# One masked 128x128 tile of probabilities per query block, and the recurrent branch in two groups, in a hybrid decoder layer

## The chip, the cores and the metric

The kernel runs as one program on one core of a Trainium2 chip. The core has a matrix engine (PE; its weight loads are shown as PEld), a vector engine (DVE), a scalar engine (ACT), a general engine (POOL, also called GpSimd) and a queue engine (SP) that mostly issues transfers; each works through its own instructions strictly in order, and the engines meet at semaphores. The metric is the device time of one execution in microseconds (us). Before the change it is 972.91 us, the median of 3 runs (972.04 to 973.18).

## The reference, cut to what matters

One decoder layer on 1024 tokens plus 16 learned meta tokens, model width 1024, all in float32:

```python
u = rmsnorm(h, g_pre_mix)
q, k, v, xr, yr = split(u @ w_in)              # 512, 128, 128, 512, 512 columns
attn = sliding_window_attention_with_sinks(q, k, v, sinks)   # 8 heads, 2 key heads
hr = rg_lru(causal_depthwise_conv(xr))         # gates, then h_t = a_t h_(t-1) + u_t
rec = gelu(yr) * hr
h = h + rmsnorm(concat(attn, rec) @ w_out, g_post_mix)
h = h + rmsnorm(relu(rmsnorm(h, g_pre_ffn) @ w_ff1)**2 @ w_ff2, g_post_ffn)
```

The attention is local. Queries and keys are cut into blocks of 128, and a query sees

```python
diff = qpos - kpos
valid = (diff >= 0) & (diff < 128) & (kpos >= PAD)   # PAD hides the padding before the meta tokens
```

So the query in row i of a block sees, of the block of keys before its own, the columns above i, and of its own block the columns up to i: 128 keys in all, except in the first real block, whose block before holds only the 16 meta tokens. Each head also has a sink, a constant logit that enters the largest value and the denominator but has no value vector.

## The kernel before

Every product is made of float32 parts: an operand is rounded to the matrix engine's format (`hi`) and the rest is kept in a second tile (`lo`); `split` (line 93) does that with a copy on ACT (line 95) and a subtraction on DVE (line 98), and `mm3` (lines 123 to 125) issues hi x hi, hi x lo and lo x hi. The program is written in the order of the text, and a scheduler sorts the instructions of each engine by readiness and priority. `behind` (line 105) and `lut` (line 81) add orders of their own: `lut` keeps all activations that need a function table in the order of the text. PSUM has four tags of two banks each: `acc`, `s`, `pt`, `o`.

The stages, with the place of each in the profiled execution:

- 0 to 60 us: `x` is loaded, normed and transposed into `u`, and the first projections (keys, values, first queries, first recurrent channel) are made, in four pieces of 256 or 272 tokens.
- about 60 to 217 us: attention in 8 units. A unit is a pair of heads (`j` of 4; head `h` = 0, 1 of the pair uses key head `h`) and a half of the tokens (4 query blocks). `scores(j, half, q)` makes the unit's probabilities, `attend(j, half, sn)` the value product, and the loop at line 604 runs `scores` of one unit, then one of the `fills` (a further projection, deferred in priority, so that it takes the matrix engine's spare time), then `attend` of the unit before.
- about 200 to 275 us: the recurrent branch in four chunks of 128 channels: `gates`, `decay`, `recur`, `rec_out`, with the last two projections (`y` chunks 2 and 3) and the first part of the output product beside them.
- from there: the output product's rest, norms, and the two feed-forward products, in which one half-size product fewer is made by sums and differences of blocks (seven of eight, both times), to 972 us.

What `scores` does for each head of a unit: for each pair of query blocks the products of 128 queries with 256 keys (hi and lo of the keys, lines 462 and 466) go to one `s` bank; for each block DVE adds a mask and takes the row's extreme in one custom instruction (line 482, 128x256), ACT makes the exponential over 257 columns, the sink's among them, and sums it (line 488, through `lut`, line 82), and DVE scales the 256 columns by the reciprocal of the sum (line 495). `attend` transposes each block's 128x256 probabilities in two matrix instructions against the identity (line 510: 4 for a bank of 2 blocks, 8 for a head and unit, 128 over the 8 units and 2 heads), splits the result, and makes the values: 10 products (line 521), since a block of keys serves the queries of its own block and of the next, 256 columns wide where it can.

In the recurrent branch, for each chunk: `gates` makes 12 products of 348 or 344 columns x 3 parts and the sigmoids; `decay` an exponential and a tanh (1040 columns each), `recur` a square root, two products on DVE and the scan along time (line 665); `rec_out(c, half)` the GeLU of `y`, the product with the state (line 671) and the split into `at[half][2 + c // 2]`. The text runs decay, decay, recur, recur for chunks 0 and 1, the same for 2 and 3, and then `rec_out` of all four for the first half, with the loads and splits of the eight 128-row pieces of `w_out` (`load_wo`, `split_wo`) between. The output product of token tile t takes the attention rows (kc 0 to 3) and the recurrent rows (kc 4 to 7, chunk c is kc 4 + c) with

```python
pos = [out_banks(t) for t in range(4)]
for t in range(4):
    out_mm(t, pos[t], range(4))
...
    out_mm(t, po, range(4 if t < 4 else 0, KC))
```

so that the attention part of tiles 0 to 3 stands ahead of the wait for the recurrent branch. `load_root` (line 170) makes one square root of a constant, which loads the table of square roots for the end of the kernel; nothing but `lut`'s order holds it.

Of the kernel before, what the change touches and what calls it, by code (L numbers as in the profile page):

```python
# [9 lines left out]
F32 = mybir.dt.float32  # L10
# [6 lines left out]
P = 128  # L17
D = 1024
KC = D // P
# [18 lines left out]
def hybrid_layer(  # L38
# [42 lines left out]
    def lut(*args, **kwargs):  # L81
        ins = nc.scalar.activation(*args, **kwargs).ins
# [8 lines left out]
        last_lut[0] = ins.name  # L91

    def split(hi, lo, src, eng=None):
# [75 lines left out]

    def load_root():  # L170
        nc.gpsimd.memset(eps_col, EPS)
        root = small.tile([P, 1], F32, name="root", tag="root")
        lut(root, eps_col, AF.Sqrt)

# [65 lines left out]
    nc.vector.tensor_copy(km.rearrange("p a b -> p (a b)"), zero)  # L240
    nc.vector.tensor_copy(vm.rearrange("p a b -> p (a b)"), zero[:, :256])

# [79 lines left out]
    def sink_k(acc, t0, n):  # L322
        o = 0
        if t0 == 0:
            m = slice(0, NMETA)
            put_k(
                [km[:, 0, m], km[:, 1, m]], [km[:, 2, m], km[:, 3, m]], acc[:, m]
            )
# [43 lines left out]
    for c in range(NLRU):  # L372
# [6 lines left out]

    mask = const.tile([P, 256], F32, name="mask")  # L380
    nc.gpsimd.memset(mask, 0.0)
    nc.gpsimd.affine_select(
        out=mask[:, 0:P], in_=mask[:, 0:P], pattern=[[1, P]], compare_op=ALU.is_gt,
        fill=NEG, base=0, channel_multiplier=-1,
    )
    nc.gpsimd.affine_select(
        out=mask[:, P:256], in_=mask[:, P:256], pattern=[[-1, P]],
        compare_op=ALU.is_ge, fill=NEG, base=0, channel_multiplier=1,
    )
    mask1 = const.tile([P, 256], F32, name="mask1")  # L390
    nc.gpsimd.memset(mask1[:, 0:P], NEG)
    nc.gpsimd.memset(mask1[:, 0:NMETA], 0.0)
    nc.gpsimd.affine_select(
        out=mask1[:, 0:NMETA], in_=mask1[:, 0:NMETA], pattern=[[1, NMETA]],
        compare_op=ALU.is_gt, fill=NEG, base=P - NMETA, channel_multiplier=-1,
    )
    nc.gpsimd.tensor_copy(mask1[:, P:256], mask[:, P:256])

# [31 lines left out]
    nc.tensor.transpose(pv[:NMETA, :P], vt[:, :NMETA], ident)  # L430
    put_v([vm[:NMETA, 0, :], vm[:NMETA, 1, :]], pv[:NMETA, :P])
    for b in range(2):
# [14 lines left out]
    def scores(j, half, q):  # L447
        sn = [slot("c", [P, 4, 257]) for _ in range(2)]
        negm = small.tile([P, 2, 4], F32, name="negm", tag="negm")
        den = small.tile([P, 2, 4], F32, name="den", tag="den")  # L450
        rden = small.tile([P, 2, 4], F32, name="rden", tag="rden")
        for h in range(2):
            nc.vector.tensor_copy(
                sn[h][:, :, 256], nsink[:, j + 4 * h : j + 4 * h + 1].to_broadcast([P, 4])
            )
        for bp in range(2):
            for h in range(2):
                sp_ = bank("s", (P, 2, 256))
# [12 lines left out]
                for i in range(2):  # L471
# [7 lines left out]
                for i in range(2):  # L479
                    b = 4 * half + 2 * bp + i  # L480
                    k = 2 * bp + i
                    nc.vector.tensor_tensor_reduce(
                        out=sn[h][:, k, 0:256], in0=sp_[:, i, :],
                        in1=mask1 if b == 0 else mask, scale=-1.0,
                        scalar=nsink[:, j + 4 * h : j + 4 * h + 1],
                        op0=ALU.add, op1=ALU.min, accum_out=negm[:, h, k : k + 1],
                    )
                    lut(
                        sn[h][:, k, :], sn[h][:, k, :], AF.Exp, scale=-1.0,
                        bias=negm[:, h, k : k + 1], accum_out=den[:, h, k : k + 1],  # L490
                    )
        for h in range(2):
            nc.vector.reciprocal(rden[:, h, :], den[:, h, :])
            for k in range(4):
                nc.vector.tensor_scalar(
                    sn[h][:, k, 0:256], sn[h][:, k, 0:256], rden[:, h, k : k + 1],
                    None, op0=ALU.mult,
                )
        return sn

    def attend(j, half, sn):
        flat = [t_.rearrange("p a b -> p (a b)") for t_ in sn]
        for h in range(2):
            ph, pl = pair("c", [P, 1024])
            for bp in range(2):
                pt = bank("pt")
                for i in range(2):
                    for s in range(2):
                        o = (2 * i + s) * P
                        nc.tensor.transpose(  # L510
                            pt[:, o : o + P],
                            sn[h][:, 2 * bp + i, s * P : (s + 1) * P], ident,
                        )
                c = slice(512 * bp, 512 * bp + 512)
                split(ph[:, c], pl[:, c], pt)
            po = bank("o")

            def av(kb, oc, n, pc, first, last):
                v = vm[:, h, :] if kb == 0 else vk[h][:, kb - 1, :]
                for k, p_ in enumerate((ph, pl)):  # L520
# [12 lines left out]
            r, o = HALF[h], HALF[1 - h]  # L533
            part, whole = flat[h][r, 0:512], flat[0][r, 512:1024]
            nc.scalar.copy(part, po[o, :])
            nc.vector.tensor_tensor(whole, po[r, :], part, op=ALU.add)
        ah, al = at[half][j // 2]
        split(ah[:, j % 2, :], al[:, j % 2, :], flat[0][:, 512:1024])

# [126 lines left out]

    def rec_out(c, half):
        o = 512 * half
        y, h = ys[c][:, o : o + 512], rg[c][0]
        lut(y, y, AF.Gelu_apprx_tanh)  # L670
        nc.vector.tensor_tensor(y, y, h[:, NMETA + o : NMETA + o + 512], op=ALU.mult)
        ah, al = at[half][2 + c // 2]
        split(ah[:, c % 2, :], al[:, c % 2, :], y)

# [27 lines left out]
    load_wo(0, "raw")  # L702
    load_wo(1, "raw")
    load_wo(2, "d")
    load_wo(3, "raw")
    split_wo(0, "ws", nc.vector)
    for kc in range(1, 4):
        split_wo(kc, "a")
    for cp in (2, 3):
        at[0][cp] = pair("b", [P, 2, 512])  # L710
    for c in range(NLRU):
        rec_out(c, 0)
    for kc in range(4, KC):
        load_wo(kc, ("d", "raw")[kc % 2])
        split_wo(kc, "a")
    for cp in (2, 3):
# [178 lines left out]
    def activate(k, q):  # L895
        t_ = fb[k][q]
        nc.scalar.activation(t_, t_, AF.Relu)
        nc.scalar.activation(t_, t_, AF.Square)
# [110 lines left out]
    for p in range(16):  # L1009
# [11 lines left out]
        if p % 2:  # L1021
            activate("22", p // 2)
            activate("12", p // 2)
        if p == 2:
# [76 lines left out]

    load_root()

# [196 lines left out]
```

## Time and profile before

| | |
|---|---|
| median of 3 runs | 972.91 us |
| the profiled execution | 974.39 us |
| its span, first to last instruction | 972.6 us |
| granted matrix-engine clock | 0.997 |
| instructions in it: PE, DVE, ACT, POOL | 4782, 995, 829, 101 |

A row of a group names the line, the engine, the operation, the tile written and the tiles read (buffer numbers left out), the shapes and the count; then the total busy time, the mean of one in ns, and the idle time of that engine just before such instructions with what ended it. A row of the timeline has the start, the time taken, and what ran; consecutive like instructions are merged, with a count. A row of a table by stretches has, for each engine, its busy time and the number of instructions, then the granted clock, the share of the transfer engines and GB/s. The matrix engine's instructions overlap (an entry's time is its way through the array), so its rate is read from the distance of starts.

### The profile page before, as it was taken

How to read it: one execution, taken by the hardware profiler on the slowest of the kernel's cores; microseconds unless marked ns; L12 is line 12 of the kernel's file. 1: busy time of each engine (PE TensorE's matmuls, PEld its weight loads, DVE VectorE, ACT ScalarE, POOL GpSimd, SP SyncE). 2: the span in 40 equal slices, each digit the busy share in tenths (PEclk: the TensorE clock that was granted, in tenths of full speed). 3: DMA queues.
4: the chain of work that ended last, by engine and by line, in shares of the span. 5: the costliest groups of instructions: out<-in, count | busy, mean ns of one | idle time of the engine just before them, and what ended most of it. 6: DMA issues, size and time to landing. Idle time of an engine off the chain costs nothing.

```text
span 972.6 us, 12482 instructions
## 1 busy us (share of the span) xinstructions
PE 953.2 (98%) x4782; PEld 801.7 (82%) x4782; DVE 672.6 (69%) x995; ACT 507.5 (52%) x829; POOL 62.5 (6%) x101
## 2 busy tenths in 40 slices
PE   6999999999999999999999999999999999999996
PEld 5999999888778887888788888888888788888885
DVE  6679997774976686665654455468567676779884
ACT  6646673567944554443555556555433343436441
POOL 4100000000002100000000000000111100001201
PEclk9999999999999999999999999999999999999998
DMA  9102101012234566576622263423777766546934
GB/s 275 44 1 66 23 23 44 23 47 69 80 111 151 154 214 202 172 254 187 205 106 87 87 215 112 127 87 110 172 173 193 171 222 200 188 150 184 250 66 87
DMA packets 87931, 129.61 MB, mean 133 GB/s; under 512 B 13592, under 2 KB 52520, under 8 KB 87872
## 3 DMA queue, kind: packets, MB, share of 16 engines
q1 hardware_dynamic: 79504, 106.54, 34.7%
q0 software_dynamic: 7936, 20.97, 10.6%
q10 hardware_dynamic: 432, 1.31, 0.4%
q8 instruction: 37, 0.61, 0.2%
q14 instruction: 22, 0.18, 0.1%
HBM read 109.93 MB, written 18.87 MB: 132 GB/s over the span
## 4 chain that ended last, share of the span: by engine, by line
PE 88%; ACT 3%; DMA 3%; DVE 3%; issue 2%; SPq 0%; DVEq 0%; ACTq 0%; POOLq 0%
PE ps_acc L124 10%; PE ps_acc L123 10%; PE ps_acc L125 10%; PE ps_pt L123 6%; PE ps_pt L125 6%; PE ps_pt L124 6%; PE ps_s L125 6%; PE ps_s L124 6%; PE ps_s L123 6%; PE ps_o L124 5%; PE ps_o L125 5%; PE ps_o L123 5%; PE ps_o L521 2%; DMA d<-in_w_ff_dram 2%; PE ps_pt L510 1%
## 5 line engine op out<-in xcount | busy, mean ns | idle before, releaser
L95 ACT CAST ws<-raw 128x1024 fp32r<-128x1024 f32 (+1 forms) x68 | 69.6, 1024 | 118.3 <-PE ps_o L124 45.2
L98 DVE TENSOR_TENSOR ws<-raw,ws 128x1024 fp32r<-128x1024 f32 (+1 forms) x69 | 82.2, 1192 | 42.6 <-ACT ws L95 42.5
L123 PE MATMUL ps_acc<-a,ws 128*128 128x256 f32 (+2 forms) x272 | 90.5, 333 | 0.6 <-DVE b L320 0.6
L124 PE MATMUL ps_acc<-a,ws 128*128 128x256 f32 (+2 forms) x272 | 89.8, 330 | 0.0
L125 PE MATMUL ps_acc<-a,ws 128*128 128x256 f32 (+2 forms) x272 | 89.4, 329 | 0.0
L95 ACT CAST ws<-e 128x1024 fp32r<-128x1024 f32 x43 | 45.0, 1048 | 65.2 <-PE ps_o L124 42.9
L98 DVE TENSOR_TENSOR b<-b,b 128x1024 fp32r<-128x1024 f32 (+2 forms) x48 | 57.5, 1199 | 26.8 <-PE ps_o L124 18.5
L95 ACT CAST b<-b 128x1024 fp32r<-128x1024 f32 (+2 forms) x48 | 49.3, 1028 | 38.5 <-DVE b L803 36.6
L98 DVE TENSOR_TENSOR ws<-e,ws 128x1024 fp32r<-128x1024 f32 x43 | 52.5, 1221 | 19.2 <-ACT ws L95 19.2
L123 PEld LDWEIGHTS ps_acc<-a,ws 128*128 128x128 f32 x272 | 51.2, 188 | 4.9 <-DVE b L320 0.8
L125 PEld LDWEIGHTS ps_acc<-a,ws 128*128 128x128 f32 x272 | 51.2, 188 | 4.6
L124 PEld LDWEIGHTS ps_acc<-a,ws 128*128 128x128 f32 x272 | 51.2, 188 | 3.9
L124 PE MATMUL ps_acc<-ws,b 128*128 128x512 f32 (+1 forms) x120 | 46.3, 386 | 0.4 <-DVE ws L98 0.4
L125 PE MATMUL ps_acc<-ws,b 128*128 128x512 f32 (+1 forms) x120 | 46.1, 384 | 0.0
L123 PE MATMUL ps_acc<-ws,b 128*128 128x512 f32 (+1 forms) x120 | 46.1, 386 | 0.0
L123 PE MATMUL ps_pt<-ws,b 128*128 128x512 f32 x112 | 44.1, 394 | 0.0
L124 PE MATMUL ps_pt<-ws,b 128*128 128x512 f32 x112 | 44.1, 393 | 0.0
L125 PE MATMUL ps_pt<-ws,b 128*128 128x512 f32 x112 | 44.0, 393 | 0.0
L123 PE MATMUL ps_s<-ws,b 128*128 128x512 f32 x110 | 43.4, 395 | 0.0
L124 PE MATMUL ps_s<-ws,b 128*128 128x512 f32 x110 | 43.3, 393 | 0.0
L125 PE MATMUL ps_s<-ws,b 128*128 128x512 f32 x110 | 43.2, 393 | 0.0
L123 PE MATMUL ps_o<-ws,b 128*128 128x512 f32 (+1 forms) x108 | 41.4, 384 | 0.0
(386 smaller groups left out, 2653.5 us busy)
## 6 DMA issues: line engine op xcount, KB each, us to landing
raw<-in_w_ff_dram SPq DMA_DIRECT2D x61, 512.0 KB, 3.8
e<-in_w_ff_dram SPq DMA_DIRECT2D x45, 512.0 KB, 3.8
d<-in_w_ff_dram SPq DMA_DIRECT2D x12, 512.0 KB, 3.8
s_dram<-d POOLq DMA_DIRECT2D x12, 512.0 KB, 3.9
raw<-in_w_in_dram SPq DMA_DIRECT2D x9, 512.0 KB, 4.0
c<-in_x_dram SPq DMA_DIRECT2D x8, 512.0 KB, 9.1
d<-in_x_dram SPq DMA_DIRECT2D x8, 512.0 KB, 4.9
out_dram<-raw SPq DMA_DIRECT2D x8, 512.0 KB, 2.6
```

Source lines behind the costliest of these rows:

```text
L95: nc.scalar.copy(hi, src)
L98: low = nc.vector.tensor_tensor(lo, src, f32(hi), op=ALU.subtract).ins
L123: nc.tensor.matmul(dst, lh, rh, start=start, stop=False, skip_group_check=True)
L124: nc.tensor.matmul(dst, lh, rl, start=False, stop=False, skip_group_check=True)
L125: nc.tensor.matmul(dst, ll, rh, start=False, stop=stop, skip_group_check=True)
L510: nc.tensor.transpose(pt[:, o : o + P], sn[h][:, 2 * bp + i, s * P : (s + 1) * P], ident,)
L521: nc.tensor.matmul(po[:, oc : oc + n], v, p_[:, pc : pc + n], start=first and k == 0, stop=last and k == 1, skip_group_check=True,)
```

## The change

**Scores.** The custom instruction and the additive masks go. ACT copies the scores of the own block (2 blocks x 128 columns) from PSUM to the tile `sn`, and DVE overwrites, where the constant tile `above` is set, with the scores of the block before. The result is one 128x128 tile for each query block, which holds every key that the query sees. For the first block a third instruction writes a large value over the padding. One DVE reduction a head and unit takes the rows' extremes, the exponentials run over 129 columns, and one DVE product scales four blocks. The sink columns are copied by POOL. The sign is carried by the query scale.

**Values.** One transpose for each block, one split for four blocks, and then POOL makes the two operands of the value products from it: `affine_select` keeps the part that belongs to the own block and, in place, the part that belongs to the block before. The 10 value products stay as they are. The 16 meta keys and values sit in the last 16 rows of their block now.

**Recurrent branch.** After `decay` and `recur` of chunks 0 and 1 come their GeLUs (both halves of the tokens), the products, splits, and two pieces of `w_out`; then the same for chunks 2 and 3. The output product of tiles 0 to 3 takes kc 4 and 5 for all four tiles, and then kc 6 and 7.

**Smaller ones.** The projections of q 3 and x 3 change places. The constant square root is put behind the squares of one of the feed-forward blocks.

```diff
-                split_scaled(q[h][r, c], q[h][o, c], acc[r], HD ** -0.5)
+                split_scaled(q[h][r, c], q[h][o, c], acc[r], -(HD ** -0.5))
...
+    above = const.tile([P, P], F32, name="above")
+    nc.gpsimd.memset(above, 1.0)
+    nc.gpsimd.affine_select(
+        out=above, in_=above, pattern=[[1, P]], compare_op=ALU.is_gt, fill=0.0, base=0,
+        channel_multiplier=-1,
     )
+    above_i = above.bitcast(mybir.dt.int32)
+    far = const.tile([P, P - NMETA], F32, name="far")
+    nc.gpsimd.memset(far, -NEG)
...
+    vmt = const.tile([P, P], F32, name="vmt")
+    nc.gpsimd.memset(vmt, 0.0)
+    nc.gpsimd.tensor_copy(vmt[:, P - NMETA :], vt[:, :NMETA])
...
     def scores(j, half, q):
-        sn = [slot("c", [P, 4, 257]) for _ in range(2)]
+        sn = slot("c", [P, 2, 4, P + 1])
...
-                    nc.vector.tensor_tensor_reduce(
-                        out=sn[h][:, k, 0:256], in0=sp_[:, i, :],
-                        in1=mask1 if b == 0 else mask, scale=-1.0,
-                        scalar=nsink[:, j + 4 * h : j + 4 * h + 1],
-                        op0=ALU.add, op1=ALU.min, accum_out=negm[:, h, k : k + 1],
+                s_ = sn[:, h, 2 * bp : 2 * bp + 2, 0:P]
+                nc.scalar.copy(s_, sp_[:, :, P:256])
+                nc.vector.copy_predicated(
+                    s_, above_i.rearrange("p (a b) -> p a b", a=1).to_broadcast([P, 2, P]),
+                    sp_[:, :, 0:P],
+                )
+                if half == 0 and bp == 0:
+                    w = slice(0, P - NMETA)
+                    nc.vector.copy_predicated(sn[:, h, 0, w], above_i[:, w], far)
+            nc.vector.tensor_reduce(
+                negm[:, h, :], sn[:, h], axis=mybir.AxisListType.X, op=ALU.min
+            )
+            for k in range(4):
+                lut(
+                    sn[:, h, k, :], sn[:, h, k, :], AF.Exp, scale=-1.0,
+                    bias=negm[:, h, k : k + 1], accum_out=den[:, h, k : k + 1],
+                )
+            nc.vector.reciprocal(rden[:, h, :], den[:, h, :])
+            nc.vector.tensor_tensor(
+                sn[:, h, :, 0:P], sn[:, h, :, 0:P],
+                rden[:, h, :].to_broadcast([P, 4, P]), op=ALU.mult,
+            )
...
+            ph, pl = (slot("c", [P, 4, 2, P], F32R) for _ in range(2))
+            pt = bank("pt")
+            for i in range(4):
+                nc.tensor.transpose(pt[:, i * P : (i + 1) * P], sn[:, h, i, 0:P], ident)
+            pt = pt.rearrange("p (a b) -> p a b", a=4)
+            split(ph[:, :, 0], pl[:, :, 0], pt)
+            for p_ in (ph, pl):
+                for s, g, op in ((1, 1, ALU.is_ge), (0, -1, ALU.is_gt)):
+                    nc.gpsimd.affine_select(
+                        out=p_[:, :, s], in_=f32(p_[:, :, 0]), pattern=[[0, 4], [g, P]],
+                        compare_op=op, fill=0.0, base=0, channel_multiplier=-g,
                     )
...
-    for kind, j in (("q", 1), ("x", 1), ("q", 2), ("x", 2), ("x", 3), ("q", 3)):
+    for kind, j in (("q", 1), ("x", 1), ("q", 2), ("x", 2), ("q", 3), ("x", 3)):
...
     for cs in ((0, 1), (2, 3)):
         for c in cs:
             decay(c)
         for c in cs:
             recur(c)
...
+        at[0][2 + cs[0] // 2] = pair("b", [P, 2, 512])
+        for c in cs:
+            for half in range(2):
+                y = ys[c][:, 512 * half : 512 * half + 512]
+                lut(y, y, AF.Gelu_apprx_tanh)
+        for c in cs:
+            rec_out(c, 0, nc.vector if c == 1 else None)
+        for kc in range(4 + cs[0], 6 + cs[0]):
+            load_wo(kc, ("d", "raw")[kc % 2])
+            split_wo(kc, "a")
...
     for t in range(4):
         out_mm(t, pos[t], range(4))
+    for t in range(4):
+        out_mm(t, pos[t], range(4, 6))
...
-        out_mm(t, po, range(4 if t < 4 else 0, KC))
+        out_mm(t, po, range(6 if t < 4 else 0, KC))
...
-    load_root()
+    load_root(squared)
```

More of the change, by code (lines that the diff above doesn't have):

```diff
@@ L91, in lut @@
         last_lut[0] = ins.name
+        return ins
     def split(hi, lo, src, eng=None):
@@ L168, in hybrid_layer, with load_root @@
     eps_col = const.tile([P, 1], F32, name="eps_col")
-    def load_root():
+    def load_root(ins):
         nc.gpsimd.memset(eps_col, EPS)
         root = small.tile([P, 1], F32, name="root", tag="root")
-        lut(root, eps_col, AF.Sqrt)
+        behind(ins.name, lut(root, eps_col, AF.Sqrt))
     def root_rstd(ssq, bias, n=P):
@@ L378, in hybrid_layer @@
     nc.vector.tensor_scalar(nsink, nsink, -1.0, None, op0=ALU.mult)
-    mask = const.tile([P, 256], F32, name="mask")
-    nc.gpsimd.memset(mask, 0.0)
+    above = const.tile([P, P], F32, name="above")
+    nc.gpsimd.memset(above, 1.0)
     nc.gpsimd.affine_select(
-        out=mask[:, 0:P], in_=mask[:, 0:P], pattern=[[1, P]], compare_op=ALU.is_gt,
-        fill=NEG, base=0, channel_multiplier=-1,
-    )
[L386 to L397, printed above, removed]
+        out=above, in_=above, pattern=[[1, P]], compare_op=ALU.is_gt, fill=0.0, base=0,
+        channel_multiplier=-1,
+    )
+    above_i = above.bitcast(mybir.dt.int32)
+    far = const.tile([P, P - NMETA], F32, name="far")
+    nc.gpsimd.memset(far, -NEG)
     lam = prm[:, :, 7]
@@ L427, in put_v @@
             split(hi, lo, src[..., HALF[h]])
+    vmt = const.tile([P, P], F32, name="vmt")
+    nc.gpsimd.memset(vmt, 0.0)
+    nc.gpsimd.tensor_copy(vmt[:, P - NMETA :], vt[:, :NMETA])
     pv = bank("o")
-    nc.tensor.transpose(pv[:NMETA, :P], vt[:, :NMETA], ident)
-    put_v([vm[:NMETA, 0, :], vm[:NMETA, 1, :]], pv[:NMETA, :P])
+    nc.tensor.transpose(pv[:, :P], vmt, ident)
+    put_v([vm[:, 0, :], vm[:, 1, :]], pv[:, :P])
     for b in range(2):
@@ L452, in scores @@
         for h in range(2):
-            nc.vector.tensor_copy(
-                sn[h][:, :, 256], nsink[:, j + 4 * h : j + 4 * h + 1].to_broadcast([P, 4])
-            )
-        for bp in range(2):
-            for h in range(2):
+            nc.gpsimd.tensor_copy(
+                sn[:, h, :, P], nsink[:, j + 4 * h : j + 4 * h + 1].to_broadcast([P, 4])
+            )
+        for h in range(2):
+            for bp in range(2):
                 sp_ = bank("s", (P, 2, 256))
@@ L478, in scores @@
                         qk(sp_[:, i, :], b, khh[h][:, c], kl[h][:, c])
[L479 to L482, printed above, removed]
-                        out=sn[h][:, k, 0:256], in0=sp_[:, i, :],
-                        in1=mask1 if b == 0 else mask, scale=-1.0,
-                        scalar=nsink[:, j + 4 * h : j + 4 * h + 1],
-                        op0=ALU.add, op1=ALU.min, accum_out=negm[:, h, k : k + 1],
[L487 to L491, printed above, removed]
@@ L492, in scores @@
-        for h in range(2):
-            nc.vector.reciprocal(rden[:, h, :], den[:, h, :])
[L494 to L498, printed above, removed]
+                s_ = sn[:, h, 2 * bp : 2 * bp + 2, 0:P]
[4 more added lines that the diff above has]
+                )
@@ L499, in scores @@
+            nc.vector.reciprocal(rden[:, h, :], den[:, h, :])
+            nc.vector.tensor_tensor(
+                sn[:, h, :, 0:P], sn[:, h, :, 0:P],
+                rden[:, h, :].to_broadcast([P, 4, P]), op=ALU.mult,
+            )
         return sn
     def attend(j, half, sn):
-        flat = [t_.rearrange("p a b -> p (a b)") for t_ in sn]
+        flat = sn.rearrange("p a b c -> p (a b c)")
+        pp = []
         for h in range(2):
[L504 to L515, printed above, removed]
+            ph, pl = (slot("c", [P, 4, 2, P], F32R) for _ in range(2))
[9 more added lines that the diff above has]
+                        compare_op=op, fill=0.0, base=0, channel_multiplier=-g,
+                    )
+            pp.append([t_.rearrange("p a b c -> p (a b c)") for t_ in (ph, pl)])
@@ L516, in attend @@
+        for h in range(2):
             po = bank("o")
@@ L519, in av @@
                 v = vm[:, h, :] if kb == 0 else vk[h][:, kb - 1, :]
-                for k, p_ in enumerate((ph, pl)):
+                for k, p_ in enumerate(pp[h]):
                     nc.tensor.matmul(
@@ L533, in attend @@
             r, o = HALF[h], HALF[1 - h]
-            part, whole = flat[h][r, 0:512], flat[0][r, 512:1024]
-            nc.scalar.copy(part, po[o, :])
-            nc.vector.tensor_tensor(whole, po[r, :], part, op=ALU.add)
+            whole = flat[r, 0:512]
+            nc.scalar.copy(whole, po[o, :])
+            nc.vector.tensor_tensor(whole, po[r, :], whole, op=ALU.add)
         ah, al = at[half][j // 2]
-        split(ah[:, j % 2, :], al[:, j % 2, :], flat[0][:, 512:1024])
+        split(ah[:, j % 2, :], al[:, j % 2, :], flat[:, 0:512])
     xc = [None] * NLRU
@@ L665, in recur, with rec_out @@
         nc.vector.tensor_tensor_scan(r, av[c], gi, 0.0, op0=ALU.mult, op1=ALU.add)
-    def rec_out(c, half):
+    def rec_out(c, half, eng=None):
         o = 512 * half
         y, h = ys[c][:, o : o + 512], rg[c][0]
-        lut(y, y, AF.Gelu_apprx_tanh)
         nc.vector.tensor_tensor(y, y, h[:, NMETA + o : NMETA + o + 512], op=ALU.mult)
         ah, al = at[half][2 + c // 2]
-        split(ah[:, c % 2, :], al[:, c % 2, :], y)
+        split(ah[:, c % 2, :], al[:, c % 2, :], y, eng)
     wo_raw = [None] * KC
@@ L701, in hybrid_layer @@
             recur(c)
[L702 to L715, printed above, removed]
+        if cs[0] == 0:
+            load_wo(0, "raw")
+            load_wo(1, "raw")
+            load_wo(2, "d")
+            load_wo(3, "raw")
+            split_wo(0, "ws", nc.vector)
+            for kc in range(1, 4):
+                split_wo(kc, "a")
[8 more added lines that the diff above has]
+            load_wo(kc, ("d", "raw")[kc % 2])
+            split_wo(kc, "a")
     for cp in (2, 3):
```

9 lines of the change are left out of this document (4 added, 5 removed).

## The prediction

> **What bounds the kernel now.** I read the page first: the busy time of each engine and the chain of work that ended last; then the busy time by stretches, and what the matrix engine waited for.
>
> ```profile
> span 972.6 us, 12482 instructions
> ...
> PE 953.2 (98%) x4782; PEld 801.7 (82%) x4782; DVE 672.6 (69%) x995; ACT 507.5 (52%) x829; POOL 62.5 (6%) x101
> ...
> PE 88%; ACT 3%; DMA 3%; DVE 3%; issue 2%; SPq 0%; DVEq 0%; ACTq 0%; POOLq 0%
> ```
>
> ```profile
> 80.00:100.00 20.00, 20.00 (x148) 18.82 (x147) 19.65 (x54) 14.60 (x36) 0.00 (x0) 1.00 0.09 27
> 240.00:260.00 20.00, 20.00 (x88) 16.23 (x87) 17.62 (x15) 19.88 (x23) 0.00 (x0) 1.00 0.25 79
> 260.00:280.00 20.00, 18.91 (x81) 14.73 (x80) 18.91 (x22) 10.84 (x16) 0.00 (x0) 1.00 0.24 77
> ```
>
> ```profile
> PE ps_pt L123 <- ACT b L95: 0.6, 1, 0.6
> PE ps_pt L125 <- DVE b L98: 0.5, 1, 0.5
> ```
>
> The matrix engine sets the time: in attention (80 to 100 us) it has no gap, although DVE is nearly as full, and POOL does nothing. Only in the recurrent branch (260 to 280 us) does it stand for 1.1 us, in the two waits of the last fence, for the split of `rec_out`. So what the change is worth is the matrix work that it takes away, less new gaps. DVE at 98% (19.65 of 20 us) is the second bound, just hidden.
>
> **The matrix work removed.** 128 transposes become 64; all other products stay (the meta values' two small transposes only get more rows). The price comes from distances of starts:
>
> ```profile
> 83.29 1.06 PE L510 MATMUL ps_pt<-ident,c 128*128 128x128 f32 x8
> 84.11 0.47 PE L124 MATMUL ps_acc<-a,ws 128*128 128x512 f32 x1
> 84.42 0.40 PE L125 MATMUL ps_acc<-a,ws 128*128 128x512 f32 x1
> 84.66 0.40 PE L123 MATMUL ps_acc<-a,ws 128*128 128x512 f32 x1
> ...
> 95.55 0.60 PE L510 MATMUL ps_pt<-ident,c 128*128 128x128 f32 x4
> 95.91 0.36 PE L462 MATMUL ps_s<-b,b 128*128 128x256 f32 x1
> 96.11 0.28 PE L466 MATMUL ps_s<-b,b 128*128 128x256 f32 x1
> 96.23 0.28 PE L462 MATMUL ps_s<-b,b 128*128 128x256 f32 x1
> ```
>
> Eight take 84.11 - 83.29 = 0.82 us, four take 0.36: 0.09 to 0.1025 each. The product right after a group takes 0.08 longer to its successor than the next one does (0.31 against 0.24; 0.20 against 0.12). 64 fewer are 5.8 to 6.6 us, middle 6.2. In the changed program's order the groups fall from 27 to 18, 9 x 0.08 = 0.7 us. Together 6.9 us, between 5.8 (if a switch costs nothing) and 7.3.
>
> **Is the matrix engine still fed in attention?** DVE and ACT by rows of 60 to 220 us:
>
> ```profile
> L482 DVE CUSTOM_DVE_ANT_0 c<-ps_s,mask,nsink 128x256 f32<-128x256 f32 x62 | 27.2, 479 | 7.1 <-PE ps_s L466 6.7
> L98 DVE TENSOR_TENSOR c<-ps_pt,c 128x512 fp32r<-128x512 f32 x32 | 21.5, 684 | 2.9 <-ACT c L95 2.7
> L495 DVE TENSOR_SCALAR c<-c,rden 128x256 f32<-128x256 f32 x64 | 18.2, 348 | 0.4
> L482 DVE DVE_READ_ACCUMULATOR2_ANT negm<- 128x1 f32 x62 | 5.0, 81 | 0.0
> L98 DVE TENSOR_TENSOR b<-ps_pt,b 128x256 fp32r<-128x256 f32 x2 | 0.8, 420 | 0.0
> ...
> L82 ACT ACTIVATE c<-c,negm 128x257 f32<-128x257 f32 x62 | 31.2, 506 | 11.8 <-DVE negm L482 11.6
> L95 ACT CAST c<-ps_pt 128x512 fp32r<-128x512 f32 x32 | 17.8, 584 | 8.4 <-PE ps_pt L510 4.1 <-DVE b L98 4.0
> L354 ACT COPY d<-ps_acc 128x256 f32<-128x256 f32 x9 | 3.4, 373 | 4.2 <-PE ps_acc L125 4.2
> ```
>
> DVE loses 27.2 + 5.0 + 18.2 us and half of 21.5, 61 us. It gains 32 predicated copies from PSUM, 16 reductions of 516 elements and 16 products of 512, none of which the trace shows. Nearest rows: 0.42 us for 256 columns out of PSUM, 0.68 for 512 columns; at worst twice that. I take them at par: 13.4 + 11 + 11 = 35 us, so DVE falls by 26 us (with doubled prices it gains 9, and would be the bound: rival below). ACT gains 32 copies of 0.37 = 11.9 us, loses 16 casts, 9.3, and its exponentials get shorter by about half their columns. Neither is on the path while the matrix engine has other work. From a head's last score product to its transposes the new order holds at least 6.7 us of matrix work; the chain there is copy 0.37, predicated copy 0.42, reduction 0.68, four exponentials of at most 0.5, reciprocal 0.17, product 0.68, with some 0.1 at each handing over: 4.9 us. It fits. The sink copies on POOL stand one unit ahead of their reduction.
>
> **The selects are the new link:** transposes, hi cast (0.58), lo (0.68), four selects of 4x128, value products; 64 selects in all. The rows that are nearest, and what happens when DVE is at work beside POOL:
>
> ```profile
> 1.26 0.28 POOL masks.py:199 TENSOR_SCALAR_AFFINE_SELECT ident<-ident 128x128 f32<-128x128 f32 x1
> 1.66 0.47 POOL L382 TENSOR_SCALAR_AFFINE_SELECT mask<-mask 128x128 f32<-128x128 f32 x1
> 2.73 0.19 POOL L393 TENSOR_SCALAR_AFFINE_SELECT mask<-mask 128x16 f32<-128x16 f32 x1
> ...
> 7.53 0.75 DVE L217 TENSOR_SCALAR d<-c,rs 128x1024 f32<-128x1024 f32 x1 [0.20 <-POOL rs L164]
> 9.05 1.52 DVE L217 TENSOR_SCALAR d<-c,rs 128x1024 f32<-128x1024 f32 x1 [0.77 <-POOL rs L164]
> 9.08 0.95 POOL L313 MEMSET b<- 64x1024 f32 x1
> 17.48 0.22 POOL L158 TENSOR_SCALAR ms<-ssq 128x1 f32<-128x1 f32 x1 [0.38 <-ACT d L215]
> 20.58 1.22 DVE L98 TENSOR_TENSOR ws<-e,ws 128x1024 fp32r<-128x1024 f32 x1
> 20.89 0.99 POOL L158 TENSOR_SCALAR ms<-ssq 128x1 f32<-128x1 f32 x1 [1.01 <-ACT d L215]
> ```
>
> From 16 to 128 columns a select grows by 0.09 (quick row) or 0.28 us (slow row); drawn on to 512 columns that is 0.19 + 496 x 0.81 ns = 0.6 us, or 1.41 us. And the two engines hold each other up: the same DVE scaling takes 1.52 instead of 0.75 us under a POOL memset, and a POOL instruction of 0.22 takes 0.99 under a DVE subtraction. About a third of attention is DVE work with two operands in SBUF (splits, convolutions, scaling), so 0.6 us grows by a third of half a microsecond or so: I take 0.8 us, nearer the quick row, since the slow one ran while DVE did.
>
> The Trainium skill (SBUF — State Buffer, section "SBUF: two separate sides") says that these two engines share a port pair as an exclusive lock, held for a whole instruction. The two pairs of rows agree. By that rule a select that always met a 1.22 us subtraction would take 1.8 us, and the sum would be a loss.
>
> What cover do they have? Counted along the new order of matrix instructions with the distances above: from a head's transposes to the first value product that needs the lo part 5.9 us at least, for 0.95 + 0.8 us of split and, behind the hi selects, four selects: at 0.8 us it ends 5.0 us after the transposes. At three places two heads' eight selects share 8 to 9 us. The first gap opens at 1.0 us a select. At 0.8: none.
>
> **Recurrent branch.** Rows for the two queues:
>
> ```profile
> 233.56 0.32 PE L125 MATMUL ps_o<-b,b 128*128 128x344 f32 x1
> ...
> 234.48 1.28 ACT L82 ACT_TABLE_LOAD   x1
> 235.77 1.16 ACT L82 ACTIVATE b<-c,m8sp 128x1040 f32<-128x1040 f32 x1
> 242.50 2.04 ACT L82 ACTIVATE c<-c 128x1040 f32<-128x1040 f32 x2
> ...
> 264.63 2.32 DVE L665 TENSOR_TENSOR_SCAN c<-b,c 128x1040 f32<-128x1040 f32 x1
> ...
> 283.31 0.40 PE L123 MATMUL ps_s<-a,b 128*128 128x512 f32 x1
> 288.63 0.39 PE L125 MATMUL ps_s<-a,b 128*128 128x512 f32 x1
> ```
>
> The clock starts when the last gate product ends (233.7 here). The matrix engine then has 159 products of 512 columns before it needs chunk 0 and 210 before chunk 3, at 5.32/23 = 0.231 us: 36.8 and 48.6 us. The other two engines, in the new order: sigmoid and table 2.0; four functions of 1.1, table, two roots, table, four GeLUs, 13; chunks 0 and 1 on DVE (two scans of 2.3, subtractions of 1.1 between) until 25; so kc 4 and 5 are early by 10 us, and both old waits (1.1 us) go. But ACT's hi cast of chunk 0 waits for DVE until 22, and the second group's table, exponentials, roots and GeLUs stand behind it: second root at 34, second scan ends at 45.8, the product at 48.8, chunk 3's cast at 49.4, its lo at 50.1. The matrix engine is there at 48.6 (lo: 49.1): a new gap of about 1.1 us, between 0 and 3. Net zero. The extra table load (1.28 us) and the four early `w_out` splits are in this sum; the load that `load_root` made in front of the splits leaves it. The `w_out` loads keep their order on SP and wait for the same freed tiles, 10 us ahead of their use. Behind the branch, the matrix order of the remaining 690 us is the same to the last instruction.
>
> **Sum.** 972.6 - 6.9 = 965.7 us of span. The profiled execution took 974.4 us, 1.5 above the median of the runs, so the median goes from 972.9 to 966.0. Its own range: 7.3 + 1.1 saved at best, 964.5; 5.8 saved and 2 us more gap at worst, 969.
>
> **Rivals.**
>
> - *The selects are slow* (slower side). One mechanism: POOL, the order's slowest link, at 1.41 us each. Carried along the order, the value products then wait 0.7 us in the first unit, 2.7 in the second, 2.9 in the fourth, 1.0 in the sixth and seventh together, 3.2 in the last: 10.5 us, 976.5. It decides from 1.3 us a select, where gaps eat the gain; at 1.9 the loss would be 30. For it: the slow row, the collisions, four rows of 128 in one pattern. Against: the quick row, and that DVE is less full than before. 0.13.
> - *Part is given back in the recurrent branch:* the start of its chain comes 7 us earlier only for the matrix engine; if ACT's queue or a `w_out` transfer is 3 us later than my sum, 969 to 970.5. For it: the 1.1 us that I find already. 0.14.
> - *Hidden anyway:* the predicated copies and reductions cost double, DVE stays at 98%, and the score chain feeds transposes late by as much as they save: 972. Against: at least 1.8 us to spare in each chain. 0.08.
>
> Forecast 0.65. The range to hold 8 in 10: 963.8 to 973.0, down to the best sum with something over, up to the hidden case; beyond it lies the slow select. Bounds of 0.2% (1.9 us, what a measurement can tell): faster 0.79 (forecast, and part given back), same 0.08, slower 0.13.
>
> **What would show it.** Right: line of the probability transposes with 64 entries; PE busy near 946; in 60 to 215 us no wait of PE for POOL; selects of 0.6 to 1.0 us; DVE near 75% there; the wait for `rec_out`'s splits, if any, on chunk 3, near 267 us. Wrong: rows of PE value products that wait for POOL, a select above 1.3 us, or waits of PE in the recurrent branch beyond 3 us.

## The result, and the profile after

The changed kernel takes 966.77 us (965.07 to 968.04, 6 runs) against 972.92 us (972.04 to 974.37, 6 runs): ratio 0.9936, 95% interval 0.9924 to 0.9949, so 6.2 us less, between 5.0 and 7.4. The forecast was 966.0.

The page of the profiled execution (966.66 us): span, busy time of the engines, shares of the chain that ended last.

```profile
span 964.8 us, 12348 instructions
...
PE 947.0 (98%) x4718; PEld 795.1 (82%) x4718; DVE 655.7 (68%) x843; ACT 504.2 (52%) x845; POOL 114.8 (12%) x179
...
PE 92%; DVE 4%; DMA 2%; ACT 0%; issue 0%; SPq 0%; DVEq 0%
```

PE has 64 instructions fewer and is busy for 953.2 - 947.0 = 6.2 us less. The span fell by 7.8 us: 6.2, the 1.1 us of the two old waits, and about half a microsecond of the first 60 us, where the input happened to land earlier. Without that last part, which varies from run to run, the profiles give 7.3 us, inside the interval of the medians; that the median of 6.2 equals the busy time alone is chance. POOL has 52 us more, DVE 17 less.

Two of the three stretches of 20 us shown for before (busy time of PE, PEld, DVE, ACT, POOL, then the granted clock):

```profile
80.00:100.00 20.00, 20.00 (x144) 18.79 (x143) 18.05 (x32) 14.93 (x50) 5.73 (x11) 1.00 0.12 27
...
260.00:280.00 20.00, 20.00 (x86) 15.65 (x85) 14.94 (x21) 7.51 (x17) 2.17 (x4) 1.00 0.37 132
```

PE is still full in attention, now also between 260 and 280 us, where it stood for 1.1 us. What PE waited for, over the whole execution, from 0.3 us up, without the waits of the first 40 us, which belong to the loading and the first projections:

```profile
PE ps_s L126 <- DVE e L99: 0.7, 1, 0.7
PE ps_acc L124 <- ACT a L994: 0.7, 1, 0.7
...
PE ps_pt L1042 <- DMA b<-t_dram: 0.3, 1, 0.3
```

No wait for POOL, and none for the recurrent branch's splits; all three lie behind 300 us. Groups of attention, 60 to 215 us:

```profile
L513 POOL TENSOR_SCALAR_AFFINE_SELECT c<-c 128x512 fp32r<-128x512 f32 x64 | 49.7, 798 | 80.1 <-ACT c L96 72.7 <-DVE c L99 5.9 <-DVE c L539 0.7
L478 DVE COPY_PREDICATED c<-above,ps_s 128x256 f32<-128x256 int32 x31 | 12.6, 448 | 2.4 <-ACT c L477 2.2
L494 DVE TENSOR_TENSOR c<-c,rden 128x512 f32<-128x512 f32 x16 | 12.2, 760 | 0.5
L485 DVE TENSOR_REDUCE negm<-c 128x4 f32<-128x516 f32 x16 | 11.0, 685 | 0.4
L508 PE MATMUL ps_pt<-ident,c 128*128 128x128 f32 x64 | 10.0, 273 | 0.0
```

The select takes 0.798 us, the predicated copy 0.45, the reduction 0.685, the product 0.76, and the transposes are 64. A quiet place of POOL's timeline, where DVE reads PSUM or one operand:

```profile
165.26 1.93 POOL L513 TENSOR_SCALAR_AFFINE_SELECT c<-c 128x512 fp32r<-128x512 f32 x3 [0.84 <-DVE c L99]
```

Three in 1.93 us are 0.64 each. The recurrent branch, by rows of the timeline (PE, then ACT and DVE, then PE):

```profile
220.82 0.32 PE L126 MATMUL ps_o<-b,b 128*128 128x344 f32 x1
...
268.54 1.28 DVE L673 TENSOR_TENSOR d<-d,c 128x512 f32<-128x512 f32 x2
...
269.25 1.23 ACT L96 CAST b<-d 128x512 fp32r<-128x512 f32 x2 [4.78 <-DVE d L673]
...
269.53 0.40 PE L126 MATMUL ps_pt<-a,b 128*128 128x512 f32 x1
269.93 0.50 PE L124 MATMUL ps_pt<-a,b 128*128 128x512 f32 x1
270.27 0.39 PE L125 MATMUL ps_pt<-a,b 128*128 128x512 f32 x1
270.66 0.50 PE L126 MATMUL ps_pt<-a,b 128*128 128x512 f32 x1
270.99 0.39 PE L124 MATMUL ps_pt<-a,b 128*128 128x512 f32 x1
```

The last gate product starts at 220.82, so the prediction's clock starts at 221.0. The hi and the lo product of chunk 3 follow 0.40 and 0.39 us after their predecessors instead of 0.23, and the four steps from 269.53 to 270.99 take 1.46 us where four take 0.92 elsewhere: the new wait is there, on chunk 3, and costs 0.5 us, which the profile counts as busy time.

### The profile page after: what moved, and what is told of

Same layout as the page of the kernel before. It is cut to its first block, busy times and chain, and to the rows that moved or that the text cites. A ratio compares the mean times of both kernels' runs of the same rounds, so it can differ in the third digit from the quotient of the medians.

```text
span 964.8 us, 12348 instructions
## 1 busy us (share of the span) xinstructions
PE 947.0 (98%) x4718; PEld 795.1 (82%) x4718; DVE 655.7 (68%) x843; ACT 504.2 (52%) x845; POOL 114.8 (12%) x179
## 4 chain that ended last, share of the span: by engine, by line
PE 92%; DVE 4%; DMA 2%; ACT 0%; issue 0%; SPq 0%; DVEq 0%
PE ps_acc L125 11%; PE ps_acc L126 11%; PE ps_acc L124 11%; PE ps_pt L126 6%; PE ps_pt L124 6%; PE ps_pt L125 6%; PE ps_s L126 6%; PE ps_s L124 6%; PE ps_s L125 6%; PE ps_o L126 5%; PE ps_o L125 5%; PE ps_o L124 5%; PE ps_o L524 2%; PE ps_s L459 1%; PE ps_s L463 1%; DMA b<-t_dram 1%
## 5 line engine op out<-in xcount | busy, mean ns | idle before, releaser
L96 ACT CAST b<-b 128x1024 fp32r<-128x1024 f32 (+2 forms) x47 | 48.8, 1038 | 37.1 <-DVE b L809 37.1
L513 POOL TENSOR_SCALAR_AFFINE_SELECT c<-c 128x512 fp32r<-128x512 f32 x64 | 49.7, 798 | 80.1 <-ACT c L96 72.7
```

The source lines that it names most:

```text
L96: nc.scalar.copy(hi, src)
L513: nc.gpsimd.affine_select(out=p_[:, :, s], in_=f32(p_[:, :, 0]), pattern=[[0, 4], [g, P]], compare_op=op, fill=0.0, base=0, channel_multip ...
```

## The experiments

Theory: the gain is the 64 transposes; grouping the recurrent branch is worth nothing; the selects have cover. The main rival: the recurrent part or one of the small edits brought the gain. Ratios are to the kernel before, timed beside each kernel on the same chip. What is said "against after" is a difference of two such ratios, and is sure to 1.5 to 2.2 us. "Idle" is the sum of PE's idle time between 60 and 300 us, by stretches of 2 us.

**Only the recurrent part** (before, with the grouping and the moved square root):

```diff
-    def rec_out(c, half):
+    def rec_out(c, half, eng=None):
...
+        for c in cs:
+            rec_out(c, 0, nc.vector if c == 1 else None)
...
+    for t in range(4):
+        out_mm(t, pos[t], range(4, 6))
...
-    load_root()
+    load_root(squared)
```

> The kernel before with the recurrent part of the change alone: two groups, output product of kc 4 and 5 ahead of 6 and 7, the constant square root put later; attention as before. Theory A (the gain is the matrix work of 64 transposes; the grouping only keeps up): no transposes go, so no gain from them. After the last gate product the new order holds only about 44 us of matrix work before it needs chunk 3, and in the changed kernel's profile chunk 3's cast was ready 48.8 us after the last gate product: a gap of about 4 us takes the place of the 1.1 us of before, 975 to 977 us. Rival B (the grouping brings a good part of the gain): 970 us or less.

Measured 975.88 us, ratio 1.0017 (1.0008 to 1.0026): slower by 1.7 us. Its waits of PE, and stretches of 2 us:

```profile
PE ps_pt L126 <- DVE b L99: 1.7, 1, 1.7
...
PE ps_pt L124 <- ACT b L96: 0.4, 1, 0.4
```

```profile
276.00:278.00 2.00, 0.61 (x3) 0.17 (x1) 2.00 (x2) 1.06 (x3) 0.00 (x0) 1.00 0.00 0
278.00:280.00 2.00, 1.42 (x5) 0.86 (x5) 2.00 (x5) 0.49 (x1) 0.00 (x0) 1.00 0.11 12
280.00:282.00 2.00, 1.82 (x4) 1.49 (x5) 2.00 (x5) 0.72 (x2) 0.00 (x0) 0.51 0.72 250
282.00:284.00 2.00, 2.00 (x7) 1.57 (x6) 0.48 (x1) 0.00 (x0) 0.00 (x0) 0.63 0.80 254
```

The new gap is 2.1 us, against 1.1 before, and behind it the granted clock falls to 0.51 and 0.63: 2 x 0.49 + 2 x 0.37 = 1.7 us more. The time is in theory A's range, but by half the gap that it named and a loss of clock that it didn't. So alone the grouping loses.

**All but the grouping** (after, with the recurrent branch of before: the reverse of the edit above, but the square root stays moved):

> The changed kernel with its recurrent branch put back as it was before (four GeLUs and products after both groups, kc 4 to 7 together); attention, load_root and the order of q 3 and x 3 as changed. Theory A: the transposes' 7 us stay; the order holds 37 us of matrix work between the last gate product and chunk 0, against 33.9 us that the wait ended at in the profile of before: no gap there, 966 to 968 us, the same as the changed kernel within 1 us. Rival B: 970 us or more.

Measured 967.32 us, ratio 0.9932 (0.9920 to 0.9944), the same as the whole change within what can be told. The recurrent branch then has two waits, of 0.3 and 0.7 us, where theory A counted none, and the clock stays at 1.00:

```profile
PE ps_pt L124 <- ACT a L96: 1.0, 2, 0.7
```

**The removed transposes put back** (after, each transpose issued twice):

```diff
             for i in range(4):
-                nc.tensor.transpose(pt[:, i * P : (i + 1) * P], sn[:, h, i, 0:P], ident)
+                for _ in range(2):
+                    nc.tensor.transpose(pt[:, i * P : (i + 1) * P], sn[:, h, i, 0:P], ident)
```

> The changed kernel with each of the 64 transposes of probabilities issued twice into the same place: the matrix work of before, but DVE, ACT and POOL as changed. Theory A: the 6 to 7 us come back, 972 to 974 us. Rival C (the gain comes from the relief of DVE, and the transposes were hidden): 967 to 968 us.

Measured 973.83 us, ratio 0.9998 (0.9989 to 1.0007). Against 0.9936 that is 0.0062 x 972.9 = 6.0 us for 64 transposes (4.5 to 7.5): the gain of the change is gone to the last part that can be measured. Between 60 and 300 us PE has no gap in this kernel, so it is the price of the work alone, and the relief of DVE by itself brings nothing.

**No selects** (after; the value products read the unmasked tile):

```diff
-            for p_ in (ph, pl):
-                for s, g, op in ((1, 1, ALU.is_ge), (0, -1, ALU.is_gt)):
-                    nc.gpsimd.affine_select(
...
-                av(kb0 + 1 + i, i * P, 256, P + 256 * i, False, False)
+                av(kb0 + 1 + i, i * P, 256, i * P, False, False)
```

> The changed kernel without the 64 selects: the value products read the unmasked tile of probabilities, so the attention's output is not the reference's. It measures what the selects cost in place. Theory A (they are covered): 966 to 967.5 us, the same within 1 us; the product that scales four blocks (128x512, two operands in SBUF), 760 ns beside the selects, falls to about 690 ns. Rival D (the selects are a link on the path, or hold DVE up enough to show): 965 us or less.

Measured 968.18 us, ratio 0.9940 (0.9925 to 0.9954), no faster than with them: the selects cost the time nothing that can be measured. What they do cost is on DVE. In this kernel, one of its groups:

```profile
L494 DVE TENSOR_TENSOR c<-c,rden 128x512 f32<-128x512 f32 x16 | 11.1, 691 | 0.5
```

The product L494, with two operands in SBUF, takes 691 ns without the selects in the kernel and 760 with them, on average. The reduction, with one, takes 683 and 685.

**Each select twice** (after):

```diff
-                    nc.gpsimd.affine_select(
+                    for _ in range(2):
+                        nc.gpsimd.affine_select(
```

> After with each of the 64 selects issued twice (the second does the same again): a mask costs POOL about 1.6 us, and POOL would be some 90 us busy with selects in attention. Theory A (the selects have cover, which ends near 1.0 us each in the changed program's order, and the scheduler of this kernel moves matrix work between them and the value products once more): counted along this kernel's own order, gaps of 2.5 us in all at 0.8 us for one issue and 12 us at 0.9, so 968 to 973, about 969, with waits of PE for POOL now in the list. Rival 1 (POOL is never on the path, the cover is far larger than my count): 967, no wait for POOL. Rival 2 (the slow select of the prediction, in the unchanged order, at 1.6 us): about 987.

Measured 976.93 us, ratio 1.0027 (1.0014 to 1.0040): 8.9 us more than after, beyond theory A's range and short of the slow rival's. A wait for POOL appears, and at its longest place the clock goes too:

```profile
PE ps_o L525 <- POOL c L514: 5.3, 4, 2.5
```

```profile
194.00:196.00 2.00, 0.81 (x5) 0.42 (x3) 1.97 (x3) 1.04 (x1) 2.00 (x2) 1.00 0.00 0
196.00:198.00 2.00, 0.72 (x5) 0.72 (x6) 2.00 (x3) 0.00 (x0) 2.00 (x4) 0.94 0.01 4
198.00:200.00 2.00, 2.00 (x9) 1.81 (x9) 0.60 (x2) 0.58 (x1) 2.00 (x4) 0.50 0.28 41
200.00:202.00 2.00, 2.00 (x8) 1.58 (x7) 0.39 (x1) 0.00 (x0) 1.14 (x2) 0.70 0.81 221
```

Idle is 5.4 us, the lost clock 2 x (0.06 + 0.50 + 0.30) = 1.7 us. My count along the order was right in kind (2.5 us at 0.8 for one issue, 12 at 0.9; here one takes 0.834), but it had no clock in it. Of the 8.9 us, 1.7 are not located.

**The masks on DVE** (after, a product with ones and zeros and a subtraction in place of the selects):

```diff
-                    nc.gpsimd.affine_select(
...
+                        nc.vector.tensor_tensor(
+                            p_[:, :, 1], f32(p_[:, :, 0]),
+                            own.rearrange("p (a b) -> p a b", a=1).to_broadcast([P, 4, P]),
+                            op=ALU.mult,
...
+                            p_[:, :, 0], f32(p_[:, :, 0]), f32(p_[:, :, 1]), op=ALU.subtract
```

> After with the masks made by DVE in place of POOL: the own part by a product with a tile of ones and zeros, the other part by a subtraction; 64 instructions of 512 columns at about 0.69 us, 44 us more on DVE, which is 80% busy between 60 and 180 us (96.5 us of 120). Theory A (DVE is the second bound, and the masks have room on POOL alone): DVE would need about 1.2 times the time that attention has, so part of the 44 us shows: 980 to 990. Rival (the matrix engine's queue of deferred work covers it whichever engine makes the masks): 966 to 968.

Measured 981.95 us, ratio 1.0079 (1.0060 to 1.0098), 13.9 us more than after, as theory A had it. The stretch from 60 to 180 us, after and then with the masks on DVE:

```profile
60.00:180.00 120.00, 120.00 (x873) 112.96 (x872) 96.54 (x162) 76.59 (x233) 47.26 (x72) 1.00 0.12 33
```

```profile
60.00:180.00 120.00, 116.10 (x823) 108.79 (x822) 114.94 (x202) 69.85 (x218) 3.39 (x12) 0.97 0.12 32
```

DVE goes from 80% to 96% busy, PE falls behind (823 instructions in the stretch instead of 873), and the clock loses 3% there. Over attention and the recurrent branch idle is 8.2 us and the lost clock 5.1, together 13.3 of the 13.9; 2.86 us of the idle stand near 236 us, in the recurrent branch, on the cast of a projection's weights on ACT. So of these two engines only POOL makes the single tile pay; masks on ACT were not tried.

**Only the square root moved** (before):

```diff
-        lut(root, eps_col, AF.Sqrt)
+        behind(ins.name, lut(root, eps_col, AF.Sqrt))
```

> Before with only the constant square root put behind the squares of a feed-forward block, as the change does. Theory A (the table load that it moves lies behind the last scan, where the matrix engine waits 1.1 us in all for the splits of the recurrent branch): at best those 1.1 us go, so ratio 0.999 to 1.000 to before. Rival (it is this edit and not the missing transposes from which some of the gain comes): ratio 0.997 or less.

Measured 972.72 us, ratio 0.9987 (0.9977 to 0.9997). PE's wait in the recurrent branch shrinks from 1.1 to 0.4 us, and stands on ACT:

```profile
PE ps_pt L124 <- ACT b L96: 0.4, 1, 0.4
```

**The old order of the last two projections** (after):

```diff
-    for kind, j in (("q", 1), ("x", 1), ("q", 2), ("x", 2), ("q", 3), ("x", 3)):
+    for kind, j in (("q", 1), ("x", 1), ("q", 2), ("x", 2), ("x", 3), ("q", 3)):
```

> After with the old order of the last two deferred projections (x 3 before q 3). Theory A (a projection is matrix work of the same length whichever comes first, and the recurrent branch starts after both): as after within 1 us, 966 to 968, ratio 0.993 to 0.995. Rival (with q 3 late, the last units' scores wait for their queries, or with x 3 early the convolution collides with the selects): 968.5 or more, with waits of PE between 150 and 217 us.

A miss: 973.29 us, ratio 0.9990 (0.9979 to 1.0000). This one line is worth 0.0054, 5.3 us, to the changed kernel. By stretches of 2 us:

```profile
150.00:152.00 2.00, 1.46 (x14) 1.22 (x12) 1.94 (x3) 0.45 (x1) 1.93 (x3) 1.00 0.00 0
152.00:154.00 2.00, 1.26 (x9) 1.12 (x9) 0.87 (x2) 0.14 (x1) 2.00 (x5) 1.00 0.00 0
154.00:156.00 2.00, 0.87 (x6) 0.88 (x7) 0.68 (x1) 1.24 (x3) 1.32 (x3) 0.90 0.00 0
156.00:158.00 2.00, 2.00 (x11) 2.00 (x11) 0.00 (x0) 0.00 (x0) 0.00 (x0) 0.50 0.00 0
158.00:160.00 2.00, 2.00 (x15) 2.00 (x15) 0.00 (x0) 0.10 (x1) 0.00 (x0) 0.75 0.03 8
```

2.4 us idle, then 2 x (0.10 + 0.50 + 0.25) = 1.7 us of clock; 1.1 us more of idle lies at 216 us and in the recurrent branch: 5.2 in all, which is the measured loss. Timeline of DVE, POOL and PE at the place:

```profile
148.12 1.28 DVE L553 SCALAR_TENSOR_TENSOR d<-d,prm,d 128x1038 f32<-128x1038 f32 x1
149.33 0.68 DVE L494 TENSOR_TENSOR c<-c,rden 128x512 f32<-128x512 f32 x1
...
150.76 1.42 DVE L553 SCALAR_TENSOR_TENSOR d<-d,prm,d 128x1037 f32<-128x1037 f32 x1
...
148.33 4.94 POOL L513 TENSOR_SCALAR_AFFINE_SELECT c<-c 128x512 fp32r<-128x512 f32 x4 [0.30 <-DVE c L99]
...
150.84 0.62 PE L508 MATMUL ps_pt<-ident,c 128*128 128x128 f32 x4
152.73 1.26 PE L524 MATMUL ps_o<-c,b 128*128 128x128 f32 x9 [1.27 <-POOL c L513]
```

The convolution of the early projection (L553) and the product L494 between its parts, all with two SBUF operands, run while four selects do, and these take 4.94 / 4 = 1.24 us each; PE has only a 256-column projection left and then waits for them.

**The new order in the kernel before:**

```diff
-    for kind, j in (("q", 1), ("x", 1), ("q", 2), ("x", 2), ("x", 3), ("q", 3)):
+    for kind, j in (("q", 1), ("x", 1), ("q", 2), ("x", 2), ("q", 3), ("x", 3)):
```

> Before with only the new order of the last two deferred projections (q 3 before x 3). The old order in the changed kernel cost it about 5 us (ratio 0.9990 against 0.9936). Theory A (that loss comes from the selects: with x 3 early its convolution stands on DVE ahead of a head's split, and the four selects behind it no longer fit; before has no selects): the swap gives before nothing, ratio 0.998 to 1.002, no wait of PE between 60 and 220 us. Rival (the swap is worth several us by itself, so that much of the change's gain is the swap and not the missing transposes): ratio 0.996 or less.

Measured 976.22 us, ratio 1.0022 (1.0013 to 1.0031): not a gain but a loss of 2.1 us. The rival falls; theory A's "nothing" was not quite right either. PE's wait, and stretches of 2 us:

```profile
PE ps_acc L123 <- ACT ws L95: 2.4, 1, 2.4
```

```profile
232.00:234.00 2.00, 0.53 (x3) 0.10 (x1) 1.29 (x2) 2.00 (x3) 0.00 (x0) 1.00 0.00 0
234.00:236.00 2.00, 1.10 (x3) 0.94 (x4) 1.12 (x1) 1.98 (x3) 0.00 (x0) 0.81 0.00 0
236.00:238.00 2.00, 2.00 (x6) 1.49 (x5) 1.94 (x3) 1.99 (x2) 0.00 (x0) 0.50 0.33 63
```

The last cast of a `y` projection's weights stands on ACT behind exponentials and tanh functions of the recurrent branch, 1.16 us each.

**The old order, without selects** (after; both edits above):

> After with the old order of the last two deferred projections and without the selects (the value products read the one unmasked tile, so the two masks are left out). Theory A (the 2.4 us for which PE stood between 150 and 156 us with the old order, and the halved clock behind it, end with the selects): the gap goes, ratio 0.993 to 0.995, what is left is at most a gap of about 0.8 us in the recurrent branch. Rival (the split of the late projection's convolution alone holds PE up, the selects only stand behind it): a gap of 1 us or more stays near 150 us, ratio 0.996 to 0.999.

Measured 969.71 us, ratio 0.9960 (0.9947 to 0.9974), between the two. Its waits of PE:

```profile
PE ps_pt L126 <- DVE b L99: 1.1, 1, 1.1
...
PE ps_acc L124 <- ACT d L354: 0.6, 1, 0.6
```

The gap near 150 us falls from 2.4 to 0.55 us and the clock stays whole, so the selects held PE up there, though the scheduler also orders the matrix work near it otherwise in this kernel. Most of the rest is the 1.1 us in the recurrent branch. None of these kernels is measurably faster than the changed one.

PE's idle and the clock explain these seven to within 1.7 us, each against the kernel named (in us; idle and clock are those of one profiled execution, the measured time is by the ratios of medians):

| kernel | idle | lost clock | sum | measured |
|---|---|---|---|---|
| recurrent part alone, against before | 2.15 - 1.09 | 1.7 | 2.8 | 1.7 |
| new order in before, against before | 2.37 - 1.09 | 1.7 | 3.0 | 2.1 |
| square root in before, against before | 0.41 - 1.09 | 0 | -0.7 | -1.3 |
| old order, against after | 3.5 | 1.7 | 5.2 | 5.3 |
| old order, no selects, against after | 1.7 | 0 | 1.7 | 2.3 |
| selects twice, against after | 5.4 | 1.7 | 7.2 | 8.9 |
| masks on DVE, against after | 8.2 | 5.1 | 13.3 | 13.9 |

## Why the prediction was right, step by step

- *What bounds the kernel, and the matrix work removed* (6.9 us, 5.8 to 7.3): right. PE's busy time fell by 6.2 us, and since 0.5 us of what is left is the stretched place in the recurrent branch, some 6.7 us of work is gone; the doubled transposes cost 6.0 (4.5 to 7.5). The 0.7 us for nine groups fewer can't be told apart from the rest.
- *Feeding PE in attention*: right. The three prices taken at par held (0.42, 0.68 and 0.68 forecast; 0.45, 0.685 and 0.76 measured), and PE has no gap. DVE, forecast near 75% between 60 and 215 us, is busy there for 117.58 of 155 us, 76%:

```profile
60.00:215.00 155.00, 155.00 (x1051) 143.28 (x1050) 117.58 (x184) 94.12 (x260) 51.57 (x76) 1.00 0.13 35
```

The page has DVE only 17 us lower where the sum had 26. By the durations of single instructions the sum is right: those that went come to 62.0 us, the predicated copies, reductions and products that came to 36.3. The copies over the padding (2.6 us), which the sum left out, and the sink copies (2.0 us), now on POOL, nearly cancel. Busy time counts an overlap once: all durations on DVE add up to about 710 us before and 688 after, the busy times to 672.6 and 655.7, so less overlaps now.

- *The selects* at 0.8 us: measured 0.798. The reason holds too: 0.64 us undisturbed (the quiet place at 165 us), 1.24 beside the convolution and a product. The first gap was put at 1.0 us a select; with a mean of 0.78 us, no longer than here, the old order of projections has a gap. So the count was right only for the one order on which it was made. What matters is not the mean but where the long selects fall.
- *Recurrent branch, net zero*: right in kind, mis-sized by 0.6 us. Both old waits (1.1 us) went, as forecast. The new gap, forecast at 1.1 us, is 0.5: chunk 3's cast begins at 269.25 and PE would have needed it at 269.8, 48.8 us after the gates as against the forecast of 48.6. So the branch gained 0.6 us instead of nothing. The grouping itself saved nothing that can be measured (0.9932 without it).
- *The smaller edits*: the prediction gave the swap of q 3 and x 3 no term. It was in the cover count, which went along the changed order, but the text didn't say that the forecast hung on it. It decides 5.3 of the 6.2 us in the changed kernel, and costs 2.1 us in the old one. The square root was a part of the recurrent sum; alone it saves 1.3 us (0.3 to 2.2).
- *The rivals.* The slow select didn't come. Its price counted a gap of 2.7 us as 2.7, and the experiments show that such a gap can cost 1.7 us of clock on top. The masks on DVE show how *hidden anyway* would have gone: with DVE at 96% the gain is more than lost.

## What to carry to other kernels

When a step is taken off the matrix engine by giving another engine a link in the chain, count that link's cover along the order that the program really has, and ask which line fixes that order: here one pair of names in a list is worth almost as much as the change. Expect a gap of two microseconds or more on the matrix engine to cost nearly twice its length, as most did here, though not all. And an edit that loses alone (the new order of projections costs the kernel before 2.1 us) can be what makes another edit pay, so take edits out of the finished kernel as well as putting them into the old one.

## What the hardware showed

A stall of PE can also take its clock. Sums of 2.0 to 2.5 us of idle within 4 to 6 us (four of the kernels above) were each followed by about 3.4 us at a clock of 0.50, 1.7 us lost. With the masks on DVE, 1.4 us of idle was followed once by about 3.4 us at half (from 199.2 us) and once by about 6.8 (from 158.3 us), with another 1.9 us of idle in the first part of that; up to 1.4 us elsewhere cost no clock. One of 2.86 us in a single piece, in the same kernel, cost none either, so length alone doesn't decide; what does was not tried. The Trainium skill (TensorE: Matmul & The Clock Gate, section "HAM oscillation — how this bites in real kernels") puts the limit for idle gaps at about 3.4 us. The half clock agrees with that section. The limit doesn't, since here shorter gaps, broken by a few products, were enough; nor does the length, about 1.67 us of throttling at a time there and 3.4 here.

A select and a DVE instruction slow each other down when the latter has two operands in SBUF (selects 0.64 to 1.24 us; the product 691 to 760 ns on average), not when it reads PSUM (the split of the transposes takes 686 ns without the selects and 684 with them), nor in the reduction, with one operand (683 and 685 ns). One operand alone doesn't spare it, though. Two rows of the same one-operand scaling in the changed kernel, and the selects beside the second:

```profile
111.21 0.81 DVE L548 TENSOR_SCALAR d<-d,prm 128x1040 f32<-128x1040 f32 x1
143.42 1.13 DVE L548 TENSOR_SCALAR d<-d,prm 128x1040 f32<-128x1040 f32 x1
...
141.70 3.35 POOL L513 TENSOR_SCALAR_AFFINE_SELECT c<-c 128x512 fp32r<-128x512 f32 x3
```

The Trainium skill (SBUF — State Buffer, section "SBUF: two separate sides") names two cases, a DVE instruction with two SBUF inputs and one in a mode that uses both ports. The trace agrees with the first; which mode the scaling ran in no run here shows.
